# Four small moves of work between engines and queues in a two-layer decoder trunk

## The chip, the cores and the metric

The kernel runs on one core of one Trainium2 chip. The metric is device time in microseconds (us) of one execution, the median of several runs. Five engines work side by side, each with its own instruction stream: TensorE (PE, matmul), VectorE (DVE), ScalarE (ACT), GpSimd (POOL) and SyncE (SP, which here only issues DMAs). They synchronise by semaphores. ACT and SP issue DMAs from their own queues, in the order of their streams.

## The reference

One inference step of a two-layer decoder trunk, in float32, for a prompt of 1024 tokens and 8 sample tokens that share the weights (1032 columns in all). The model width is 1024, the width of the feed-forward part 3072.

```
for l in range(2):
    hn = rmsnorm(x, norm_mix_g[l])
    if l == 0:  main = rglru(conv4(hn @ w_in_a)) * gelu(gate)
    else:       main = window-128 attention over the shared K/V
    mo = memory attention (4 heads, 256 positions)
    x = x + concat(main, mo) @ w_out[l]
    hn = rmsnorm(x, norm_ffn_g[l])
    x = x + conv_ffn(hn, state, w_ffn_up[l], cw, cb, w_ffn_down[l])
    if l == 0:  k_sh, v_sh = shared_kv(x)

def conv_ffn(x, buf, w_up, cw, cb, w_down):
    u = x @ w_up
    u, nbuf = causal_dwconv(u, buf, cw, cb)      # three taps along the tokens
    return (gelu(u[..., :3072]) * u[..., 3072:]) @ w_down, nbuf
```

For a sample token the two earlier columns of the conv come from a saved state, and the last two columns of the prompt and each sample's column are outputs too (`nbuf`).

## The kernel before

**Layout.** Activations lie transposed: 128 features on the partitions, 1032 token columns along the free dimension. A `row` is one tile of 128 x 1032 float32, `sm` and `ty` are smaller ones. `ul` collects the tails of the conv: for each of the 48 up tiles the last two prompt columns and the eight sample columns.

**Matmuls in three passes.** Every float32 operand is split into a high part in a shorter format (`acopy`, made by ACT) and a low part (the difference, made by POOL with `gtt` or DVE with `vtt`). `mm3` (lines 298 to 303) multiplies high x high, high x low and low x high. In the trace these are lines 301, 302 and 303. Lines 108, 116, 119 and 122 are the one-line helpers `act`, `vtt`, `gtt` and `stt`, so most of the work of ACT, DVE and POOL has the line of a helper.

**Up projection.** For each of 24 column tiles `j` of the feed-forward part, `ffn` computes a gate and a value tile together, by seven products of half-sized blocks in place of eight (`STEADY` order P1, P6, P2, P7, P5, P4, P3). `combine` makes the weight of each product from the raw halves: POOL adds or subtracts two 128x512 halves (not for all), ACT copies the high part, POOL subtracts for the low part. The products' sums are added by DVE and copied by ACT into the gate row `ug` and the value row `uv`. After P4 the value row, and after P3 the gate row, is scaled by the norm factor on DVE (`scale`). `post(j)` is a generator that continues one step at each product: conv row of the value (`act_conv`, ACT, with the tail copy), two taps (`taps`, DVE, 128x1023 and 128x1022), the same for the gate, then gelu (ACT), the product of both (DVE), and the store to DRAM (`gD`, by ACT's queue). So a round of one `j` has four taps and two tail copies. After every twelfth `j`, `samples` computes the sample columns from `ul` with four POOL operations, a gelu and a POOL product, and stores them to `gD`.

**Down projection.** While the last column tile is computed, `fetch(i)` loads the first six gated rows back from `gD` and `gated(i)` splits them (high on ACT, low on DVE). The down weights are split by `get` (which loads with `load_w` what is not yet loaded). `down(c, m, b)` then accumulates chunks of six tiles.

**Mixer of layer 1 and its out projection.** Attention results go to DRAM (`mD`). `load_m(b)` loads column block `b` (384, 384 and 264 columns) back and splits it. `start_m(b)` starts that as a task, `mgetB` is asked for a block by the out projection and starts it if it isn't running, then finishes it.

**What sets the order.** The Tile framework schedules DVE, POOL, PE and SP from the program's text; ACT, except in layer 1's mixer, keeps the order in which the program is written. `tick()` advances each running task (`spawn`) by one step. Waits stand in the engine's stream, so what follows a waiting instruction on the same engine or queue waits too.

Of the kernel before, what the change touches and what calls it, by code (L numbers as in the profile page):

```python
# [16 lines left out]
SEQ = 1024  # L17
NB = 8
NT = SEQ + NB
# [10 lines left out]
TIL = ((0, 1, 2), (3, 4, 5), (6, 7))  # L30
# [6 lines left out]
DCH = 6  # L37
SG = 12
# [14 lines left out]
def tile_trunk(ctx: ExitStack, tc: tile.TileContext, I: dict, O: list):  # L53
    nc = tc.nc
    mul, add, sub, amax = ALU.mult, ALU.add, ALU.subtract, ALU.max
# [22 lines left out]
    def row(dt=F32):  # L78
        return rp.tile([P, NT], dt, tag="row", name=nm("row"))
# [30 lines left out]
    def acopy(out, in_, **kw):  # L110
        return act(out, in_, AF.Copy, **kw)

    V, G, T, SY = nc.vector, nc.gpsimd, nc.tensor, nc.sync

    def vtt(out, a, b, op):
        return V.tensor_tensor(out=out, in0=a, in1=b, op=op)  # L116
# [12 lines left out]
    def f(ap):  # L129
        return ap.bitcast(F32)  # L130
# [22 lines left out]
    def spawn(g):  # L153
        t = Task(g)
        tasks.append(t)
        return t
# [75 lines left out]
    gD = dp.tile([2, KF, P, NT], F32, name="gD")  # L232
# [6 lines left out]
    widx = {}  # L239
# [10 lines left out]
    def w_load(i):  # L250
        u = W[i]
        u["raw"] = row()
        a, b = u["shape"]
        SY.dma_start(u["raw"][:, : a * b].rearrange("p (a b) -> p a b", a=a), u["src"])
# [18 lines left out]
    def get(key, ahead=1, load=1):  # L273
        i = widx[key]
        if Prep.fences and i >= Prep.fences[0]:
            Prep.fences.pop(0)
        end = (Prep.fences[0] if Prep.fences else len(W)) - 1
        top = min(end, i + ahead)
        while Prep.split <= top:
            while Prep.loaded <= min(end, Prep.split):  # L280
                w_load(Prep.loaded)
                Prep.loaded += 1
            w_split(Prep.split)
            Prep.split += 1
        while Prep.loaded <= min(end, top + load):
            w_load(Prep.loaded)
            Prep.loaded += 1
        return W[i]["t"]

    def load_w(n):  # L290
        while Prep.loaded < n:
            w_load(Prep.loaded)
            Prep.loaded += 1
# [588 lines left out]
    def ffn(l, ops, need, factor, weights, on_block, store=None):  # L882
        ul3 = ul.rearrange("p (c t) -> p c t", c=10)
# [7 lines left out]
        def act_conv(u, t):  # L891
            a = row()
            act(a[:, :SEQ], u[:, :SEQ], AF.Identity, scale=fwc(2, t), bias=fbc(t))
            G.tensor_copy(out=ul3[:, :, t], in_=u[:, SEQ - 2 : NT])  # L894
            return a

        def taps(a, u, t):
# [23 lines left out]
        def samples(j0):  # L921
            pair = []
            for t0 in (j0, KF + j0):
                t = sm()[:, : 8 * SG].rearrange("p (b j) -> p b j", b=8)
                w = fw[:, None, 2 * MU + t0 : 2 * MU + t0 + SG].to_broadcast([P, 8, SG])
                gtt(t, ul3[:, 2:10, t0 : t0 + SG], w, mul)
                gtt(t, t, sb3[:, :, t0 : t0 + SG], add)
                pair.append(t)
            act(pair[0], pair[0], AF.Gelu_apprx_tanh)
            o = sm()[:, : 8 * SG].rearrange("p (j b) -> p j b", b=8)  # L930
            gtt(o.rearrange("p j b -> p b j"), pair[0], pair[1], mul)
            SY.dma_start(gD[l, j0 : j0 + SG, :, SEQ:NT].rearrange("j p b -> p j b"), o)

        def product(j, name, hfs):
            w = made[j, name]
# [46 lines left out]
        gh, gl, ga = {}, {}, {}  # L982
# [5 lines left out]
        def gated(j):  # L988
            a = ga.pop(j)
            gh[j], gl[j] = row(F32R), row(F32R)  # L990
            acopy(gh[j][:, :NT], a[:, :NT])
            vtt(gl[j][:, :NT], a[:, :NT], f(gh[j][:, :NT]), sub)

        def refill(m):
            x[m] = row()
# [6 lines left out]
        for q, (j, name, hfs) in enumerate(SEQUENCE):  # L1002
            if q == 2:
                load_pair(1)
            if q == 8:
                factor()
            want = 7 + max(0, q - 4) // 2 if q < 14 else min(len(todo), q - 7 + AHEAD)
            while at < want:
                combine(*todo[at])
                at += 1  # L1010
            t = product(j, name, hfs)
            if t is not None:
                last.append(t)
            tick()
            if j == KF - 1:
                i = STEADY.index(name)
                if i < DCH:
                    fetch(i)
                if i > 1:
                    gated(i - 2)  # L1020
                if i == 4:
                    get(f"dn{l}.0.0", 0, 1)

        def down(c, m, b):
# [275 lines left out]
    for i in range(9):  # L1300
        np_ = P if i < 8 else NB
        p = ps()
# [15 lines left out]
    for key in ORDER_A:  # L1318
        t = int(key[1])
# [279 lines left out]
    for j, i in enumerate(order0):  # L1599
        p = ps()  # L1600
# [82 lines left out]
    for i in range(9):  # L1683
        p = ps()
# [15 lines left out]
    swa_done = set()  # L1700
# [133 lines left out]
    sst = None  # L1834
    for e in range(2):
        qu = [get(f"q{e}.{u}", 0, 1) for u in range(4)]
        for j, i in enumerate(order2):
            np_ = P if i < 8 else NB
            p = ps()
            tm(p, 18 + 9 * e + j, qu, 2, 384)  # L1840
            t = start(q_post(p, np_, i, e))
            if i == 8 and e == 1:
# [4 lines left out]
                sst = bgadd(sample_swa(bm96))  # L1847
# [23 lines left out]
    mload = {}  # L1871

    def start_m(b):
        if b not in mload:
            while not {(i, e) for i in TIL[b] for e in range(2)} <= swa_done:
                tick()
            if b == 2:
                bgfinish(sst)
            mload[b] = spawn(load_m(b))
# [7 lines left out]

    x = {}
    start_m(0)
    get("out1.0.0", 1, 1)  # L1890
    for _ in range(6):
        tick()
# [139 lines left out]
```

## Time and profile before

| | us |
|---|---|
| median of 3 runs | 2558.35 |
| the three runs | 2557.54, 2558.35, 2558.95 |
| profiled execution, its own time | 2557.26 |
| profiled execution, span | 2555.5 |
| mean granted TensorE clock | 0.971 |
| busy: PE, DVE, ACT, POOL | 2344.0, 1703.8, 1120.4, 1541.3 |
| up projection layer 0, layer 1 | about 480 to 975, 1780 to 2270 |
| out projection of layer 1 | about 1625 to 1750 |

The span is the time from the first to the last instruction in the trace; times in the trace count from its start. In the rows below a bracket such as [0.60 <-ACT row L108] says that the engine sat idle for 0.60 us before the instruction, until ACT finished a `row` at line 108. The clock is in parts of full speed: 1.00 is 2.4 GHz, 0.50 is 1.2 GHz. "x2" joins two instructions that follow each other; their common time runs from the first's start to the last's end. An instruction's time includes what it waits inside the engine.

### The profile page before, as it was taken

The page shows a single profiled execution, that of the slowest core. Times are in us where ns is not written, and L with a number is a line of the kernel's source. Part 1 is how long each engine was busy: PE and PEld are TensorE (multiplying, and loading weights), DVE is VectorE, ACT ScalarE, POOL GpSimd, SP SyncE. Part 2 cuts the span into 40 slices and gives each one's busy share as a digit, 9 for nine tenths or more (in the row PEclk, how much of TensorE's full clock was granted, in tenths as well). Part 3 has the DMA queues.
Part 4 walks back from the last instruction along what each step waited for, and adds up shares of the span by engine and source line. Part 5 has one row for each costly group of instructions (what it writes and reads, how often), then busy time and mean ns, then how long its engine had stood idle before and what let it go on. Part 6 is the DMA issues. An engine that isn't in the chain of part 4 may idle for free.

```text
span 2555.5 us, 42979 instructions
## 1 busy us (share of the span) xinstructions
PE 2344.0 (92%) x16590; PEld 2250.7 (88%) x16590; DVE 1703.8 (67%) x2772; ACT 1120.4 (44%) x2313; POOL 1541.3 (60%) x1103
## 2 busy tenths in 40 slices
PE   7998879999999998999989987779999999989999
PEld 5898769999999998999977877779999899989999
DVE  6659976777777777332487799777777777773321
ACT  5667865433333334211365577554333333342110
POOL 2149855689999995222144446355899989963220
PEclk9999889999999999999989999889999999999999
DMA  4221134212222216332665553542122222154211
GB/s 162 86 68 46 62 133 135 75 67 75 75 75 75 75 67 236 100 100 76 198 222 161 176 172 105 163 141 94 68 71 71 74 75 72 70 197 147 95 58 64
DMA packets 151132, 273.66 MB, mean 107 GB/s; under 512 B 37184, under 2 KB 93072, under 8 KB 150928
## 3 DMA queue, kind: packets, MB, share of 16 engines
q1 hardware_dynamic: 134800, 237.29, 28.2%
q10 hardware_dynamic: 16128, 33.63, 3.4%
q8 instruction: 131, 2.15, 0.3%
q14 instruction: 73, 0.60, 0.1%
HBM read 211.99 MB, written 58.87 MB: 106 GB/s over the span
## 4 chain that ended last, share of the span: by engine, by line
PE 32%; POOL 30%; issue 13%; DVE 11%; ACT 5%; DMA 1%; SPq 0%; POOLq 0%; ACTq 0%; DVEq 0%
POOL row L119 27%; PE ps L303 10%; PE ps L301 10%; PE ps L302 10%; ACT row L108 4%; DVE row L116 3%; POOL ul L894 2%; DVE row L122 2%; DVE sm L116 2%; DVE ty L116 1%; ACT sm L108 1%; POOL sm L119 1%; DVE ty L399 1%; DVE row L1209 1%; DVE ty L122 0%
## 5 line engine op out<-in xcount | busy, mean ns | idle before, releaser
L301 PE MATMUL ps<-row,row 128*128 128x258 f32 (+4 forms) x5032 | 1512.7, 302 | 47.9 <-ACT row L108 42.8
L303 PE MATMUL ps<-row,row 128*128 128x258 f32 (+4 forms) x5032 | 1493.3, 301 | 49.0 <-POOL row L119 48.7
L302 PE MATMUL ps<-row,row 128*128 128x258 f32 (+4 forms) x5032 | 1508.2, 301 | 26.1 <-DVE row L116 19.0
L119 POOL TENSOR_TENSOR row<-row,row 128x512 fp32r<-128x512 f32 (+9 forms) x666 | 1105.7, 1671 | 688.6 <-ACT row L108 381.5
L301 PEld LDWEIGHTS ps<-row,row 128*128 128x128 f32 x5032 | 957.6, 190 | 71.3 <-ACT row L108 48.4
L303 PEld LDWEIGHTS ps<-row,row 128*128 128x128 f32 x5032 | 951.2, 191 | 67.7 <-POOL row L119 60.8
L302 PEld LDWEIGHTS ps<-row,row 128*128 128x128 f32 x5032 | 958.7, 191 | 40.7 <-DVE row L116 22.4
L108 ACT ACTIVATE row<-row 128x512 fp32r<-128x512 f32 (+9 forms) x688 | 487.3, 738 | 980.5 <-POOL row L119 369.8
L116 DVE TENSOR_TENSOR row<-row,ps 128x258 f32<-128x258 f32 (+2 forms) x672 | 287.2, 444 | 467.7 <-PE ps L303 464.8
L116 DVE TENSOR_TENSOR row<-row,row 128x1032 f32<-128x1032 f32 (+8 forms) x286 | 388.8, 1371 | 110.9 <-ACT row L108 95.3
L122 DVE SCALAR_TENSOR_TENSOR row<-row,fw,row 128x1023 f32<-128x1023 f32 x192 | 349.8, 1841 | 60.9 <-POOL ul L894 47.8
L108 ACT ACTIVATE row<-ps 128x258 f32<-128x258 f32 (+6 forms) x430 | 157.7, 406 | 75.7 <-PE ps L303 26.3
L119 POOL TENSOR_TENSOR row<-row,ty 128x768 f32<-128x768 f32 (+2 forms) x56 | 77.1, 1377 | 165.7 <-DVE ty L416 62.6
L119 POOL TENSOR_TENSOR row<-row 128x512 f32<-128x512 f32 x96 | 163.3, 1701 | 6.7
L108 ACT ACTIVATE row<-row,fw 128x1024 f32<-128x1024 f32 x96 | 114.2, 1230 | 13.1 <-DVE row L116 13.1
L116 DVE TENSOR_TENSOR sm<-sm,sm 128x258 f32<-128x258 f32 (+5 forms) x125 | 90.2, 724 | 32.1 <-ACT sm L108 29.2
L108 ACT ACTIVATE row<-ps,ty,ty 128x256 f32<-128x256 f32 (+1 forms) x160 | 87.4, 563 | 9.1 <-DVE ty L116 7.0
L108 ACT ACTIVATE sm<-ps 128x384 f32<-128x384 f32 (+5 forms) x156 | 65.1, 444 | 41.0 <-PE ps L434 23.7
L116 DVE TENSOR_TENSOR row<-ps,row 128x384 fp32r<-128x384 f32 (+2 forms) x125 | 63.4, 518 | 18.7 <-ACT sm L108 8.4
L894 POOL COPY ul<-row 128x10 f32<-128x10 f32 x96 | 67.8, 706 | 9.2 <-DVE row L116 9.2
L119 POOL TENSOR_TENSOR sm<-sm,row 128x192 f32<-128x192 f32 (+3 forms) x72 | 48.9, 694 | 37.8 <-DVE sm L116 18.3
L122 DVE SCALAR_TENSOR_TENSOR row<-sm,pack,row 128x384 f32<-128x384 f32 (+1 forms) x54 | 59.1, 1097 | 14.0 <-POOL row L127 13.4
(171 smaller groups left out, 1586.8 us busy)
## 6 DMA issues: line engine op xcount, KB each, us to landing
row<-in_w_ffn_up SPq DMA_DIRECT2D x96, 512.0 KB
row<-gD SPq DMA_DIRECT2D x48, 516.0 KB
gD<-row ACTq DMA_DIRECT2D x48, 512.0 KB
row<-in_w_ffn_down SPq DMA_DIRECT2D x64, 384.0 KB
row<-hD SPq DMA_DIRECT2D x48, 512.0 KB
row<-in_w_out SPq DMA_DIRECT2D x32, 512.0 KB
rD<-sm ACTq DMA_DIRECT2D x64, 129.0 KB
row<-rD SPq DMA_DIRECT2D x16, 516.0 KB
```

What stands on the lines that cost most here:

```text
L108: return nc.scalar.activation(out, in_, func, **kw)
L116: return V.tensor_tensor(out=out, in0=a, in1=b, op=op)
L119: return G.tensor_tensor(out=out, in0=a, in1=b, op=op)
L122: return V.scalar_tensor_tensor(out=out, in0=a, scalar=s, in1=b, op0=op0, op1=op1)
L301: T.matmul(out, ah, bh, start=first and j == 0, stop=False, skip_group_check=more)
L302: T.matmul(out, ah, bl, start=False, stop=False, skip_group_check=more)
L303: T.matmul(out, al, bh, start=False, stop=last and j == n - 1, skip_group_check=more)
L399: V.tensor_reduce(out=mx[:, c0 : c0 + m], in_=s3, axis=AX.X, op=amax, negate=True)
L894: G.tensor_copy(out=ul3[:, :, t], in_=u[:, SEQ - 2 : NT])
L1209: V.tensor_tensor_scan(out=y[:, s], data0=r[:, s], data1=gx[:, s], initial=init, op0=mul, op1=add)
```

## The change

Five edits. (A) The tail copies into `ul` go from POOL to ACT, right behind the conv row. (B) Of the first six gated rows of each layer, the low part of rows 0, 2 and 4 is made by POOL and no longer by DVE. (C) The store of the sample columns goes from SP's queue to ACT's. (D) The first two down weights are loaded three products earlier, and the first one is split one product later. (E) In layer 1 a task started with the out projection's first block watches for the attention results of blocks 1 and 2 and starts their loads as soon as these are there, not when the out projection asks for them.

```diff
         def act_conv(u, t):
             a = row()
             act(a[:, :SEQ], u[:, :SEQ], AF.Identity, scale=fwc(2, t), bias=fbc(t))
-            G.tensor_copy(out=ul3[:, :, t], in_=u[:, SEQ - 2 : NT])
+            acopy(ul3[:, :, t], u[:, SEQ - 2 : NT])
             return a
...
             gtt(o.rearrange("p j b -> p b j"), pair[0], pair[1], mul)
-            SY.dma_start(gD[l, j0 : j0 + SG, :, SEQ:NT].rearrange("j p b -> p j b"), o)
+            nc.scalar.dma_start(gD[l, j0 : j0 + SG, :, SEQ:NT].rearrange("j p b -> p j b"), o)
...
             acopy(gh[j][:, :NT], a[:, :NT])
-            vtt(gl[j][:, :NT], a[:, :NT], f(gh[j][:, :NT]), sub)
+            (gtt if j < DCH and j % 2 == 0 else vtt)(gl[j][:, :NT], a[:, :NT], f(gh[j][:, :NT]), sub)
...
                 if i > 1:
                     gated(i - 2)
-                if i == 4:
+                if i == 1:
+                    load_w(widx[f"dn{l}.0.0"] + 2)
+                if i == 5:
                     get(f"dn{l}.0.0", 0, 1)
...
     x = {}
     start_m(0)
+
+    def ask_m():
+        for b in (1, 2):
+            while b not in mload:
+                if {(i, e) for i in TIL[b] for e in range(2)} <= swa_done and (b == 1 or sst.done):
+                    start_m(b)
+                else:
+                    yield
+
+    spawn(ask_m())
     get("out1.0.0", 1, 1)
```

What POOL has in its stream in one regular round of layer 0's up projection before, from the low part of one product's weight to that of a later one (`ul_102` is the tail tile, `row_967` and `row_971` the value and gate row of the round):

```order
L119 TENSOR_TENSOR row_979_6200<-row_954_5899,row_979_6200 128x512
L894 COPY ul_102<-row_967_6064 128x10
L119 TENSOR_TENSOR row_980_6230<-row_954_5899,row_980_6230 128x512
L119 TENSOR_TENSOR row_954_5899<-row_954_5899 128x512
L894 COPY ul_102<-row_971_6098 128x10
L119 TENSOR_TENSOR row_983_6269<-row_955_5901,row_983_6269 128x512
L119 TENSOR_TENSOR row_987_6303<-row_955_5901,row_987_6303 128x512
L119 TENSOR_TENSOR row_991_6337<-row_954_5899,row_991_6337 128x512
```

And the same place on POOL with the change, and below it ACT's stream there:

```order
L119 TENSOR_TENSOR row_979_6200<-row_954_5899,row_979_6200 128x512
L119 TENSOR_TENSOR row_980_6230<-row_954_5899,row_980_6230 128x512
L119 TENSOR_TENSOR row_954_5899<-row_954_5899 128x512
L119 TENSOR_TENSOR row_983_6269<-row_955_5901,row_983_6269 128x512
L119 TENSOR_TENSOR row_987_6303<-row_955_5901,row_987_6303 128x512
L119 TENSOR_TENSOR row_991_6337<-row_954_5899,row_991_6337 128x512
```

```order
L108 ACTIVATE row_980_6230<-row_954_5899 128x512
L108 ACTIVATE row_981_6260<-row_967_6064,fw_100 128x1024
L108 ACTIVATE ul_102<-row_967_6064 128x10
L108 ACTIVATE row_982_6265<-row_971_6098,fw_100 128x1024
L108 ACTIVATE ul_102<-row_971_6098 128x10
L108 ACTIVATE row_983_6269<-row_955_5901 128x512
```

The two copies have left POOL, and the split that stood behind the second (`row_983`) now follows the combine directly; on ACT each copy stands behind its conv row. The rest of the round is in the same order on every engine.

SP's stream before, where the loads of block 2 (`row_2928` and on, from `mD_88`) stand, behind the loads of out weights and of the residual (`xD_87`):

```order
L254 DMA row_2925_18542<-in_w_out 128x1024
L564 DMA row_2926_18544<-xD_87 128x124
L565 DMA row_2926_18544<-xD_87 128x3x128
L568 DMA row_2926_18544<-xD_87 128x8
L564 DMA row_2926_18544<-xD_87 128x124
L565 DMA row_2926_18544<-xD_87 128x3x128
L568 DMA row_2926_18544<-xD_87 128x8
L1860 DMA row_2928_18552<-mD_88 128x2x128 x2
L1860 DMA row_2929_18560<-mD_88 128x2x128 x2
L1860 DMA row_2930_18568<-mD_88 128x2x128 x2
L1860 DMA row_2931_18576<-mD_88 128x2x128 x2
```

And with the change, from the last attention store of layer 1 on:

```order
L1714 DMA mD_88<-sm_2841_18009 128x384
L1862 DMA row_2861_18119<-mD_88 128x2x128 x2
L254 DMA row_2864_18127<-in_w_out 128x1024
L1862 DMA row_2869_18169<-mD_88 128x2x128 x2
L1862 DMA row_2874_18212<-mD_88 128x2x128 x2
L254 DMA row_2877_18220<-in_w_out 128x1024
L560 DMA row_2878_18222<-xD_87 128x4x128
L561 DMA row_2878_18222<-xD_87 128x4
L560 DMA row_2878_18222<-xD_87 128x4x128
L561 DMA row_2878_18222<-xD_87 128x4
L1862 DMA row_2886_18280<-mD_88 128x2x128 x2
```

The eight loads of block 2 moved ahead, to right behind the last attention store and in among the out weights and residual rows of the first half; before, some twenty other DMAs stood between that store and them. The twelve loads of block 1 stand where they stood.

POOL at the end of layer 0's up projection, with the change (128x1032 are the low parts of gated rows 0, 2 and 4; 128x768 those of down weights; 128x96 and 128x8x12 the samples):

```order
L119 TENSOR_TENSOR row_1319_10329<-row_1280_9887,row_1319_10329 128x512
L119 TENSOR_TENSOR row_1322_10362<-row_1311_10287,row_1321_10361 128x1032
L119 TENSOR_TENSOR row_1330_10429<-row_1320_10359,row_1329_10428 128x1032
L119 TENSOR_TENSOR row_1335_10466<-row_1317_10324,row_1334_10465 128x768
L119 TENSOR_TENSOR sm_1344_10520<-ul_102,fw_100 128x96
L119 TENSOR_TENSOR sm_1345_10523<-ul_102,fw_100 128x96
L119 TENSOR_TENSOR sm_1344_10520<-sm_1344_10520,sb_101 128x96
L119 TENSOR_TENSOR sm_1345_10523<-sm_1345_10523,sb_101 128x96
L119 TENSOR_TENSOR row_1339_10505<-row_1328_10426,row_1338_10504 128x1032
L119 TENSOR_TENSOR sm_1346_10527<-sm_1344_10520,sm_1345_10523 128x8x12
L119 TENSOR_TENSOR row_1350_10537<-row_1318_10326,row_1349_10536 128x768
```

Before, the three rows of 128x1032 stood on DVE, two tail copies stood behind the 128x768 split, and the sample product followed the four sample operations directly.

## Rows read from the trace of the kernel before

**Rows 1.** The page, part 1: busy time, share of the span, instructions.
```profile
PE 2344.0 (92%) x16590; PEld 2250.7 (88%) x16590; DVE 1703.8 (67%) x2772; ACT 1120.4 (44%) x2313; POOL 1541.3 (60%) x1103
```

**Rows 2.** Stretches: us; busy of PE, PEld, DVE, ACT, POOL; PEclk; DMA share, GB/s.
```profile
480.00:975.00 495.00, 469.82 (x3808) 460.44 (x3808) 366.40 (x388) 193.97 (x325) 451.96 (x300) 1.00 0.22 75
1690.00:1704.00 14.00, 4.71 (x22) 4.71 (x23) 13.06 (x17) 7.29 (x17) 10.05 (x9) 0.51 0.39 116
```

**Rows 3.** The page, part 5: groups (count | busy us, mean ns | idle before, releaser).
```profile
L303 PE MATMUL ps<-row,row 128*128 128x258 f32 (+4 forms) x5032 | 1493.3, 301 | 49.0 <-POOL row L119 48.7
...
L894 POOL COPY ul<-row 128x10 f32<-128x10 f32 x96 | 67.8, 706 | 9.2 <-DVE row L116 9.2
```

**Rows 4.** Timeline of one round, DVE (start us, duration us, instruction, [idle before]).
```profile
614.27 2.27 DVE L122 SCALAR_TENSOR_TENSOR row<-row,fw,row 128x1023 f32<-128x1023 f32 x1 [1.33 <-POOL ul L894]
616.58 2.20 DVE L122 SCALAR_TENSOR_TENSOR row<-row,fw,row 128x1022 f32<-128x1022 f32 x1
616.58 3.39 DVE L122 SCALAR_TENSOR_TENSOR row<-row,fw,row 128x1022 f32<-128x1022 f32 x2
...
620.56 1.66 DVE L122 SCALAR_TENSOR_TENSOR row<-row,fw,row 128x1022 f32<-128x1022 f32 x1
...
635.81 2.27 DVE L122 SCALAR_TENSOR_TENSOR row<-row,fw,row 128x1023 f32<-128x1023 f32 x1 [1.33 <-POOL ul L894]
```

**Rows 5.** Timeline of the same round, POOL.
```profile
615.54 2.15 POOL L119 TENSOR_TENSOR row<-row 128x512 f32<-128x512 f32 x1
617.64 1.20 POOL L894 COPY ul<-row 128x10 f32<-128x10 f32 x1
618.79 4.58 POOL L119 TENSOR_TENSOR row<-row,row 128x512 fp32r<-128x512 f32 x2
623.97 3.08 POOL L119 TENSOR_TENSOR row<-row,row 128x512 fp32r<-128x512 f32 x2 [0.60 <-ACT row L108]
```

**Rows 6.** Timeline of the same round, ACT.
```profile
611.89 1.16 ACT L108 ACTIVATE row<-row 128x512 fp32r<-128x512 f32 x2 [4.36 <-POOL row L119]
...
622.31 1.58 ACT L108 ACTIVATE row<-row 128x1024 f32<-128x1024 f32 x2 [5.42 <-DVE row L122]
```

**Rows 7.** Timeline of a round halfway, DVE (first three) and POOL.
```profile
745.84 6.55 DVE L122 SCALAR_TENSOR_TENSOR row<-row,fw,row 128x1023 f32<-128x1023 f32 x3 [3.55 <-ACT row L108]
...
752.98 1.63 DVE L122 SCALAR_TENSOR_TENSOR row<-row,fw,row 128x1022 f32<-128x1022 f32 x1
...
768.20 2.27 DVE L122 SCALAR_TENSOR_TENSOR row<-row,fw,row 128x1023 f32<-128x1023 f32 x1 [1.33 <-POOL ul L894]
...
747.78 1.28 POOL L119 TENSOR_TENSOR row<-row 128x512 f32<-128x512 f32 x1
749.02 4.50 POOL L119 TENSOR_TENSOR row<-row,row 128x512 fp32r<-128x512 f32 x2
756.36 1.83 POOL L119 TENSOR_TENSOR row<-row,row 128x512 fp32r<-128x512 f32 x1 [2.83 <-ACT row L108]
```

**Rows 8.** Tile `ul`: who waited for it (us, times).
```profile
DVE row L122: 47.8, 36
```

**Rows 9.** Timeline at block 2 of layer 1's out projection, PE, SP, POOL.
```profile
1699.29 0.58 PE L301 MATMUL ps<-row,row 128*128 128x258 f32 x1 [12.65 <-ACT row L108]
...
1690.86 4.72 SPq L1860 DMA_DIRECT2D row<-mD  x8
...
1689.61 4.48 POOL L119 TENSOR_TENSOR row<-row,row 128x516 fp32r<-128x516 f32 x2
```

**Rows 10.** Timeline from up to down, layer 0, PE and DVE.
```profile
987.38 0.45 PE L302 MATMUL ps<-row,row 128*128 128x384 f32 x1 [1.69 <-DVE row L116]
...
994.90 0.69 PE L301 MATMUL ps<-row,row 128*128 128x384 f32 x1 [3.63 <-ACT row L108]
...
988.57 1.42 DVE L116 TENSOR_TENSOR row<-row,row 128x1032 fp32r<-128x1032 f32 x1
```

**Rows 11.** Groups of POOL, by form (count | busy us, mean ns | idle before).
```profile
L119 POOL TENSOR_TENSOR row<-row,row 128x1032 f32<-128x1032 f32 x6 | 14.9, 2488 | 9.6 <-ACT row L108 5.7 <-DVE row L122 3.8
```

## The prediction

> **What bounds the kernel now.** I read the shares by engine, then one stage of each kind by stretches, then the timeline of one round of the long stage on POOL, DVE and ACT, and last the idle times of PE. PE is busy for 92% of the span, so at first sight little is left [rows 1]. But in the stage that matters most, the up projections (480 to 975 us in layer 0, and its like in layer 1), POOL is busy for 451.96 of 495 us [rows 2], and PE's matmuls of the third kind (line 303) wait 48.7 us in all for POOL's rows [rows 3]. POOL looks like the second bound.
>
> The timeline of one round says otherwise. A round is one of the 24 column tiles of a layer. It repeats from the first tap at 614.27 to the next at 635.81: 21.54 us [rows 4]. In it no engine is full; they wait for each other in a ring. ACT starts its pair at 611.89 after 4.36 us idle, waiting for POOL, and then makes the two conv rows. DVE's four taps run from 614.27 to 620.56 + 1.66 = 622.22. ACT starts the gelu at 622.31 after 5.42 us idle, waiting for DVE. POOL starts its next series at 623.97 after 0.60 us idle, waiting for ACT [rows 4 to 6]. So a round is the sum of POOL's series, DVE's four taps (7.95 us) and ACT's pieces between them. What is removed from POOL outside that sum only makes its idle longer.
>
> Inside the four taps DVE and POOL hold each other up. POOL's 128x512 instruction takes 2.15 us at 615.54, while the same form took 1.28 us at 747.78 [rows 5, 7]. Taps 1 and 2 take 2.27 and 2.20 us; taps 2 and 3 together take 3.39, so tap 3 adds only 1.19 [rows 4]. They take turns: each waits for the other's instruction that is running. The Trainium skill (SBUF - State Buffer, "Who interferes with whom") calls this pair of ports an exclusive lock, held for the whole instruction; the trace agrees with its 2.15 against 1.28 us.
>
> **Part A, the tail copies to ACT.** The copies are 96, with a mean of 706 ns on POOL, 67.8 us in all [rows 3]. The two of a round take 1.41 us, of which the second takes 1.20 [rows 5]. But that copy is mostly waiting: it begins at 617.64 and ends at 618.84, just after tap 2 ends at 616.58 + 2.20 = 618.78. It has POOL's turn and does almost nothing with it, and so tap 3 runs right behind tap 2, unhindered. The order shows that after the change POOL's next split stands there. It takes the turn at 618.78, holds it, and tap 3 has to wait, as taps 1 and 2 do.
>
> What that costs has two prices. By counting turns, tap 3 goes from 1.19 to the 2.27 us of tap 1: +1.08 per round. The other price is measured: in one round halfway, from 745.84, the copies happen to fall before the second tap, and splits stand where the second copy otherwise is. There the first three taps take 6.55 us instead of 614.27 to 619.97 (5.70), and the four last from 745.84 to 752.98 + 1.63 = 754.61, 8.77 us (against 7.95: +0.82). POOL's idle time before its next series grows from 0.60 to 2.83 us, and the next round begins 22.36 us later (768.20) instead of 21.54 [rows 4, 5, 7]. That is the pattern that I expect everywhere. I take 0.88, a quarter of the way from the measured 0.82 to the counted 1.08.
>
> Regular rounds are those whose first tap waits 1.33 us with the copy as the last to come; there are 36 [rows 4, 8]. 36 x 0.88 = **+31.7 us** (29.5 to 38.9). The other 12 (first and last rounds of a layer, and the two that have the pattern already) I take at nothing.
>
> The copies on ACT: no row shows this form there. POOL's first copy of a round took 1.41 - 1.20 = 0.21 us, and two of that lie in ACT's idle 5.42 us [rows 6]; cost nothing. Were that cover gone, 0.21 on the path of 36 rounds would be +7.6.
>
> **Part E, the watcher.** Block 2 of layer 1's out projection finds PE idle for 12.65 us until 1699.29. SP issues that block's eight loads only from 1690.86 [rows 9]. The order shows them now ahead, among the weight loads of the first half; block 1's loads stay where they were, and so does its wait. At most the whole idle time goes, and with it the slow matmuls behind it: from 1690 to 1704 the granted clock is 0.51, and 22 matmuls take 4.71 us, 0.214 each, where the long stage has 469.82 / 3808 = 0.123 [rows 2]; 22 x 0.09 = 2.0. So at most -14.7. What is late next: the low half of the block's second weight, which POOL finishes at 1689.61 + 4.48 = 1694.09 [rows 9]. PE would come from 1686.64 and have 48 matmuls (two tiles of 24) on the first weight, 5.9 us, until 1692.5: a wait of 1.6. I allow three such waits in the block's eight tiles: **-9.9 us**. A loss is not excluded: the eight issues, 4.72 us, now stand ahead of weight loads on SP, and ACT, in written order, may wait for a landing; so +4.7 to -14.7.
>
> **Parts B, C, D, the change from up to down in each layer.** PE waits there 1.69 us for DVE's last splits and 3.63 us for ACT (layer 0) [rows 10]. B moves three of the six splits to POOL, 2.49 us each there (from the nearest form, 128x1032) against 1.42 on DVE [rows 10, 11]. The order puts two of them before the first weights' low half, which is covered by DVE's own splits, and the third behind four sample operations and ahead of the sample product. With C, ACT's queue waits for that product before it can split the next down weight, for which PE already waits 3.63 us. I take two differences of 2.49 - 1.42 = 1.07 on the path per layer, **+4.3 us** in two layers. Ends: both waits vanish, 2 x (1.69 + 3.63) = -10.6; two whole POOL splits are added, 2 x 2 x 2.49 = +10. D's earlier load and later split move under work that PE has anyway: nothing. The Trainium skill (Perfetto Trace Analysis, "Optimizing Scalar/DVE Operations") says that moving work between DVE and GpSimd might not help; by that this part would be 0 and the sum 2579. No row shows these splits on POOL at this place.
>
> **Sum.** 2557.26 (the profiled execution; the median of the runs is 1.1 higher) + 31.7 - 9.9 + 4.3 = 2583.4: **2583 us**.
>
> **Rivals.**
> 1. *POOL is the bound* and the copies' time comes back. For: its 451.96 of 495 us and PE's 48.7 us of waits for it [rows 2, 3]. 36 x 1.41 = 50.8, capped by those 48.7: 2557.3 - 48.7 - 9.9 + 4.3 = 2503. Against: POOL waits for ACT in each round, and where its copies were out of the way its idle grew by 2.2 us and the round did not shrink [rows 5, 7]. 5%. The Trainium skill (Perfetto Trace Analysis, "Optimizing GPSIMD Operations") says to prefer other engines over GpSimd where possible; by that rule this rival would win.
> 2. *The turn is not taken*: the split behind the copy waits for a row of ACT. It decides at 618.78: if ACT's row (now behind two copies) comes later than that, tap 3 runs free and the round stays at 21.54. Then only E and the transitions count: 2557.3 - 9.9 + 4.3 = 2552, faster. Against: that split starts at 618.79 with no idle time before it [rows 5]. 11%.
> 3. *The bubble only moves*: A as forecast, but ACT or SP passes the wait on to the first half. 2557.3 + 31.7 + 4.3 = 2593. For it: ACT takes its queue in order. 19%.
>
> **How the numbers follow.** The forecast has 63%, the rivals 35, mishaps at either end 2. About 0.2% (5 us) can be told from no change. The bounds of the forecast are not all met at once: E and the transitions at their better ends with A at its lower make 2561, and A at its upper with E at nothing and the transitions at +10 make 2606. From 2558 to 2601 the range leaves out rivals 1 and 2 and a little at the top. Faster by over 0.2%: rival 1 and half of rival 2, 0.11. Within: the other half and the lowest of the forecast, 0.07. Slower: 0.82.
>
> **What would show it.** Right: rounds of 22.4 us; tap 3 at 2.2 us or more; POOL's idle time before its series near 2.8 us; PE's waits for POOL longer, not shorter; no copies in POOL's rows and 96 on ACT of about 0.2 us; the idle time at block 2 down to a few us, block 1's wait still there. Wrong: rounds of 21.5 with tap 3 near 1.2 (rival 2), rounds near 20.2 with POOL free of idle time (rival 1), or new PE waits for ACT between 1640 and 1690 (rival 3).

## The result and the profile after

The changed kernel takes 2600.6 us (median of 4 runs, 2597.30 to 2608.73), the kernel before 2558.65 in the same comparison: ratio 1.0169, 95% interval [1.0145, 1.0193], or +37 to +49 us. Slower was forecast, but by 26 us. The time lies at the very end of the range, and the ratio's middle, 2558.65 x 1.0169 = 2602, just beyond it.

The page's first part, of the profiled execution (2608.73 us, the slowest of the four, 8 us above their median; all rows of the changed kernel are from it):

```profile
PE 2365.1 (91%) x16590; PEld 2265.4 (87%) x16590; DVE 1735.7 (67%) x2766; ACT 1129.2 (43%) x2409; POOL 1501.6 (58%) x1013
```

POOL lost 40 us of work against [rows 1], and the time rose. One regular round of layer 0, timeline, DVE first, then POOL, ACT and PE (start us, duration us, instruction, [idle before]):

```profile
619.97 6.63 DVE L122 SCALAR_TENSOR_TENSOR row<-row,fw,row 128x1023 f32<-128x1023 f32 x3 [1.33 <-ACT ul L108]
...
627.19 1.63 DVE L122 SCALAR_TENSOR_TENSOR row<-row,fw,row 128x1022 f32<-128x1022 f32 x1
...
642.42 6.62 DVE L122 SCALAR_TENSOR_TENSOR row<-row,fw,row 128x1023 f32<-128x1023 f32 x3 [1.33 <-ACT ul L108]
...
626.52 0.74 DVE L116 TENSOR_TENSOR row<-row,ps 128x258 f32<-128x258 f32 x2
...
621.11 2.15 POOL L119 TENSOR_TENSOR row<-row 128x512 f32<-128x512 f32 x1
623.22 4.52 POOL L119 TENSOR_TENSOR row<-row,row 128x512 fp32r<-128x512 f32 x2
630.57 4.45 POOL L119 TENSOR_TENSOR row<-row,row 128x512 fp32r<-128x512 f32 x3 [2.83 <-ACT row L108]
...
619.77 0.20 ACT L108 ACTIVATE ul<-row 128x10 f32<-128x10 f32 x1
...
628.91 1.58 ACT L108 ACTIVATE row<-row 128x1024 f32<-128x1024 f32 x2 [6.13 <-DVE row L122]
...
626.99 0.39 PE L301 MATMUL ps<-row,row 128*128 128x258 f32 x1 [0.88 <-DVE row L116]
```

The first three taps take 6.63 us where they took 5.70 [rows 4]; all four take 627.19 + 1.63 - 619.97 = 8.85, before 7.95. POOL's split follows its combine at 623.22 with no copy between. POOL then idles 2.83 us before its next series, before 0.60 [rows 5], and the next round's taps begin 22.45 us later, before 21.54. It is the picture of the halfway round [rows 7] in the regular rounds. The copies on ACT take 0.20 us each and cost nothing, as the second experiment shows.

The longer round reaches PE through DVE. Right behind the third tap DVE adds two matmul results (`ps`, 128x258, at 626.52) to their rows, and PE, which waits for the first of these sums, stands still for 0.88 us. In the round of [rows 4] PE has no such wait. In the whole program it shows at line 301, first before, then after (count | busy us, mean ns | idle before, releasers):

```profile
L301 PE MATMUL ps<-row,row 128*128 128x258 f32 (+4 forms) x5032 | 1512.7, 302 | 47.9 <-ACT row L108 42.8 <-DVE row L116 4.0 <-PE ps L397 1.0
...
L301 PE MATMUL ps<-row,row 128*128 128x258 f32 (+4 forms) x5032 | 1519.2, 304 | 73.6 <-DVE row L116 37.1 <-ACT row L108 36.4
```

PE's waits there for DVE's rows grew from 4.0 to 37.1 us, while those for POOL at line 303 stayed, 48.7 [rows 3] before and 47.9 after.

To place the time, I took from each trace when the n-th matmul starts (the same matmul in all kernels, except that neighbours are swapped in up to some 400 of the 16590 places) and summed differences to the kernel before by stage, in us. "Up" and "to down" are the up projection and the change from up to down of layers 0 and 1, "mixer B" is what lies between layer 0's down projection and layer 1's out projection; the down stages, not shown, moved by 0.2 at most in layer 0 and 0.4 in layer 1.

```
profiled execution       start   up 0  to down 0  mixer B  out proj 1   up 1  to down 1
changed kernel            -1.6   21.4     5.0       3.7      -2.0       19.4     5.5
A alone                   -2.7   20.1    -0.4       1.8       4.5       17.6     1.2
A and an extra copy       -4.0   -1.2    -0.1      -2.8       0.4        0.7     0.3
E alone                   -2.9    0.0    -0.2      -1.5      -5.8        2.6     0.3
E, later                  -3.0   -0.1    -0.2      -1.7      -9.5        2.2    -0.7
E, low parts on POOL      -2.6    0.0     0.0      -0.6      -3.1        1.6    -0.8
B, C, D                   -2.3    0.3     6.2      -1.4      -0.3        1.4     8.1
B alone                   -2.7    1.1     6.6       2.2       4.2        0.0     6.8
C alone                   -0.7    0.3     4.2      -2.0       5.4        0.9     3.5
rows 0 and 2, C, D        -2.2    1.0     6.2       0.0       4.9        0.9     6.4
E later, rows 0 and 2     -0.3    0.3     0.1      -0.9      -9.5        1.7     0.8
changed, two undone       -3.4   20.1     1.7       0.4      -1.1       18.2     2.1
```

The start and the mixer are the same work in all of these, and vary by up to 4 and 6.5 us; differences below that, in these two columns, mean nothing. Where nothing in them was changed, the up stages repeat within 3 us and the changes to down within 2.

The out projection varies by 5 us even where nothing in it was changed, and this has a place. In seven of the thirteen traces (the changed kernel; A; B; C; rows 0 and 2, C, D; E, low parts on POOL; changed, two undone) its first 85 matmuls take 3.9 to 5.5 us longer than in the kernel before. In these seven PE, some 40 matmuls into the stage, waits 1.8 to 2.1 us for DVE, and in or right behind that wait the granted clock falls to 0.50. In the other traces these matmuls differ by 0.5 us at most. An example of the wait, then the 6.7 us around and behind it, and the same place with E alone (us; PE busy (matmuls), PEclk, DMA share, GB/s):

```profile
1640.97 0.58 PE L302 MATMUL ps<-row,row 128*128 128x258 f32 x1 [2.04 <-DVE row L116]
1640.20:1646.90 6.70, 5.38 (x23) 0.50 0.11 40
...
1638.20:1644.90 6.70, 6.70 (x52) 1.00 0.37 108
```

From the 86th matmul to the end of the out projection all kernels without part E agree with the kernel before within 0.1 us, and those with it gain 6.3 (E alone), 5.9 (changed kernel and changed, two undone), 9.5 (E, later), 9.4 (E later, rows 0 and 2) and 8.6 us (E, low parts on POOL).

The out projection of layer 1 (timeline; DVE, ACT, PE):

```profile
1698.71 4.69 DVE L116 TENSOR_TENSOR row<-row,row 128x264 fp32r<-128x264 f32 x4
1703.33 0.41 DVE L116 TENSOR_TENSOR sm<-row,ps 128x258 f32<-128x258 f32 x1
...
1703.77 0.51 ACT L108 ACTIVATE row<-sm,pack 128x258 f32<-128x258 f32 x1 [5.68 <-DVE sm L116]
...
1705.59 0.58 PE L301 MATMUL ps<-row,row 128*128 128x258 f32 x1 [5.61 <-ACT row L108]
```

The 12.65 us before block 2 [rows 9] are gone, and a wait of 5.61 us stands in the first half, where there was none of that size. Following the chain back: PE waits for a weight's high part on ACT; ACT, in written order, stands before a sum's scaling that waits for DVE; DVE makes four of block 2's low parts first (4.69 us).

The change from up to down, layer 0 (PE, then POOL, then DVE and ACT):

```profile
1013.86 0.69 PE L302 MATMUL ps<-row,row 128*128 128x384 f32 x1 [5.92 <-POOL row L119]
...
1020.52 0.45 PE L301 MATMUL ps<-row,row 128*128 128x384 f32 x1 [2.26 <-ACT row L108]
...
1006.28 2.54 POOL L119 TENSOR_TENSOR sm<-ul,fw 128x96 f32<-128x96 f32 x2 [4.57 <-ACT ul L108]
1008.78 2.70 POOL L119 TENSOR_TENSOR sm<-sm,sb 128x96 f32<-128x96 f32 x2
1011.44 2.36 POOL L119 TENSOR_TENSOR row<-row,row 128x1032 fp32r<-128x1032 f32 x1
...
1015.92 0.56 DVE L116 TENSOR_TENSOR row<-row,ps 128x384 f32<-128x384 f32 x1 [4.69 <-PE ps L303]
...
1019.62 4.22 ACT L108 ACTIVATE row<-row 128x768 fp32r<-128x768 f32 x5 [7.06 <-DVE row L116]
```

POOL makes row 4's low part (128x1032) only after four sample operations, and PE waits 5.92 us for it. DVE's sums then wait for PE, the last gated row behind these sums, and ACT's next weight behind that row's store. Before, PE waited 1.69 and 3.63 us here [rows 10].

### The profile page after: what moved, and what is told of

Same layout as the page of the kernel before. It is cut to its first block, busy times and chain, and to the rows that moved or that the text cites. A ratio compares the mean times of both kernels' runs of the same rounds, so it can differ in the third digit from the quotient of the medians.

```text
span 2606.9 us, 43020 instructions
## 1 busy us (share of the span) xinstructions
PE 2365.1 (91%) x16590; PEld 2265.4 (87%) x16590; DVE 1735.7 (67%) x2766; ACT 1129.2 (43%) x2409; POOL 1501.6 (58%) x1013
## 5 line engine op out<-in xcount | busy, mean ns | idle before, releaser
L301 PE MATMUL ps<-row,row 128*128 128x258 f32 (+4 forms) x5032 | 1519.2, 304 | 73.6 <-DVE row L116 37.1
L119 POOL TENSOR_TENSOR row<-row,row 128x512 fp32r<-128x512 f32 (+11 forms) x672 | 1124.3, 1686 | 784.2 <-ACT row L108 461.1
L302 PE MATMUL ps<-row,row 128*128 128x258 f32 (+4 forms) x5032 | 1515.8, 303 | 31.7 <-DVE row L116 15.4
L303 PE MATMUL ps<-row,row 128*128 128x258 f32 (+4 forms) x5032 | 1498.9, 302 | 48.1 <-POOL row L119 47.9
L116 DVE TENSOR_TENSOR row<-row,row 128x1032 f32<-128x1032 f32 (+8 forms) x280 | 381.4, 1373 | 96.8 <-ACT row L108 79.0
L122 DVE SCALAR_TENSOR_TENSOR row<-row,fw,row 128x1023 f32<-128x1023 f32 x192 | 387.8, 2040 | 71.4 <-ACT ul L108 51.9
L122 DVE SCALAR_TENSOR_TENSOR row<-sm,pack,row 128x384 f32<-128x384 f32 (+1 forms) x54 | 59.8, 1111 | 14.0 <-POOL row L127 13.4
L108 ACT ACTIVATE row<-sm,pack 128x258 f32<-128x258 f32 x64 | 32.4, 507 | 74.6 <-DVE sm L116 74.6
```

Source lines behind the costliest of these rows:

```text
L108: return nc.scalar.activation(out, in_, func, **kw)
L119: return G.tensor_tensor(out=out, in0=a, in1=b, op=op)
L122: return V.scalar_tensor_tensor(out=out, in0=a, scalar=s, in1=b, op0=op0, op1=op1)
L301: T.matmul(out, ah, bh, start=first and j == 0, stop=False, skip_group_check=more)
L302: T.matmul(out, ah, bl, start=False, stop=False, skip_group_check=more)
L303: T.matmul(out, al, bh, start=False, stop=last and j == n - 1, skip_group_check=more)
```

## The experiments

**Part A alone.** One line of the kernel before, nothing else.

```diff
-            G.tensor_copy(out=ul3[:, :, t], in_=u[:, SEQ - 2 : NT])
+            acopy(ul3[:, :, t], u[:, SEQ - 2 : NT])
```

> Part A alone (the 96 tail copies on ACT, nothing else changed). Turn theory: the split takes the turn that the copy left unused, so the 36 regular rounds go from 21.53 to 22.42 us, third tap 2.3 in place of 1.27, and the total rises by 30 to 34: about 2590. Rival (POOL is the bound and gets its time back): about 2508. Rival (the change's loss comes from its other parts): 2558.

Measured: 2597.82, ratio 1.0154 [1.0139, 1.0169], +39 us. The taps:

```profile
619.00 6.62 DVE L122 SCALAR_TENSOR_TENSOR row<-row,fw,row 128x1023 f32<-128x1023 f32 x3 [1.33 <-ACT ul L108]
...
641.43 4.38 DVE L122 SCALAR_TENSOR_TENSOR row<-row,fw,row 128x1023 f32<-128x1023 f32 x2 [1.33 <-ACT ul L108]
```

Rounds of 22.43 and slow third taps, as the turn theory says; the rivals fall. But the total rose by 39 us and not by 30 to 34, and the up stages by 37.7, not by 36 x 0.89 = 32.0. By the first taps' starts the first round of layer 0 takes 23.67 in place of 21.42 and the last that can be measured 23.12 in place of 21.59; with their like in layer 1 these add 7.1 us, and I had put them at nothing. The fourth round of layer 0, one of the 36, takes 23.68 in place of 21.53, and the twelfth round of each layer, also of the 36, shrinks by 0.4.

**Part A and an extra copy that nothing needs.** This is the direct test: only the turn is given back, not the work.

```diff
+            acopy(ul3[:, :, t], u[:, SEQ - 2 : NT])
-            G.tensor_copy(out=ul3[:, :, t], in_=u[:, SEQ - 2 : NT])
...
             ag = act_conv(ug, j)
+            G.tensor_copy(out=ty()[:, :10], in_=ug[:, SEQ - 2 : NT])
```

> Part A, and beside it one extra copy of 10 columns on POOL into a tile that nothing reads, where the second tail copy stood. Turn theory: a copy with no work gives DVE its turn back; third tap 1.27, rounds 21.53, total 2558 within 3. Rival (the two copies on ACT lengthen the ring, or the conv row is read by two engines): rounds stay at 22.4 and the total at 2590.

Measured: 2559.47, ratio 0.9997 [0.9984, 1.0011].

```profile
611.66 5.56 DVE L122 SCALAR_TENSOR_TENSOR row<-row,fw,row 128x1023 f32<-128x1023 f32 x3 [1.33 <-ACT ul L108]
...
614.90 1.19 POOL L909 COPY ty<-row 128x10 f32<-128x10 f32 x1
616.05 4.58 POOL L119 TENSOR_TENSOR row<-row,row 128x512 fp32r<-128x512 f32 x2
621.22 4.46 POOL L119 TENSOR_TENSOR row<-row,row 128x512 fp32r<-128x512 f32 x3 [0.59 <-ACT row L108]
```

The useless copy takes 1.19 us on POOL, three taps are back at 5.56, POOL idles 0.59 us again, and the next round's taps start at 633.06, 21.40 later. PE's waits at line 301 for DVE's rows are 2.7 us in all, where A alone has 38.3. All of part A's loss is the lost turn; ACT's copies cost nothing. This agrees with the exclusive lock on the ports that DVE and GpSimd share, of which the Trainium skill tells (SBUF - State Buffer, "Who interferes with whom"); that the two engines take turns by the instruction is what the traces add.

**Part E alone.** The watcher, as in the change, in the kernel before.

```diff
     start_m(0)
+    def ask_m():
...
+    spawn(ask_m())
```

> Part E alone (the watcher). Theory 1 (the wait only moves: block 2's low parts on DVE delay the first half's sums, and the in-order ACT with them): the 12.65 us at block 2 go, new waits of 5 us or more appear in the first half, total 2554 to 2557. Theory 2 (E is good for its full 10 us, and what was lost was lost to other parts of the change): total about 2548 and no new wait over 3 us in the first half.

Measured: 2553.66, ratio 0.9981 [0.9970, 0.9991]. As in theory 1 the wait moves, in the same chain as above:

```profile
1662.51 4.69 DVE L116 TENSOR_TENSOR row<-row,row 128x264 fp32r<-128x264 f32 x4
...
1667.57 0.51 ACT L108 ACTIVATE row<-sm,pack 128x258 f32<-128x258 f32 x1 [5.65 <-DVE sm L116]
...
1669.38 0.58 PE L301 MATMUL ps<-row,row 128*128 128x258 f32 x1 [5.66 <-ACT row L108]
```

The out projection gains 5.8 us in this trace, 6.3 behind its first 85 matmuls; by the runs E is worth 5 us (2 to 8).

**The watcher, later.** Part E, with block 2 held back for four more steps.

```diff
                 if {(i, e) for i in TIL[b] for e in range(2)} <= swa_done and (b == 1 or sst.done):
+                    if b == 2:
+                        for _ in range(4):
+                            yield
                     start_m(b)
```

> Part E alone, with the watcher holding block 2 back for four more steps. Theory 1 (the splits of block 2 on DVE, ahead of the first half's sums, hold ACT's queue and through it PE; later they do it less): the new wait in the first half shrinks below 4 us, block 2 still finds its rows ready, total 2549 to 2553. Theory 2 (the wait comes from the loads standing ahead of weight loads on SP): no change against the watcher alone, 2553 to 2556, or the 12.65 us come back in part.

Measured: 2548.24, ratio 0.9970 [0.9958, 0.9982], faster than the kernel before and the changed one, by 0.3% against the kernel before.

```profile
1670.61 0.39 PE L301 MATMUL ps<-row,row 128*128 128x258 f32 x1 [1.49 <-ACT row L108]
```

That is the longest wait left in the first half, apart from the one that starts the stage, and 1.50 us stood there before too. Block 2 still finds its rows. So it is where block 2's work stands, not that it is done early, that cost the difference: 5.8 us are gained in the out projection with the watcher as it is, 9.5 with the later one. The difference rests on the traces; the two ratios' intervals overlap. The four steps hold back the loads as well as the splits, and the next experiment tells them apart.

**Block 2's low parts on POOL.** Part E, with the low parts of block 2 made by POOL.

```diff
-                vtt(Ml[k][:, c0 : c0 + n], r3[:, e], f(Mh[k][:, c0 : c0 + n]), sub)
+                (gtt if b == 2 else vtt)(Ml[k][:, c0 : c0 + n], r3[:, e], f(Mh[k][:, c0 : c0 + n]), sub)
```

> Part E alone, with block 2's eight low parts made by POOL in place of DVE. Theory 1 (DVE's queue carries the wait into the first half): the wait of 5 to 7 us there shrinks to under 3, total 2548 to 2553. Theory 2 (SP's queue or ACT's high parts carry it): it stays, total 2553 to 2557, or worse by POOL's slower splits.

Measured: 2552.53, ratio 0.9980 [0.9970, 0.9989]. The wait of 5.66 us is gone, but PE now waits for POOL there:

```profile
1672.60 0.39 PE L303 MATMUL ps<-row,row 128*128 128x258 f32 x1 [1.94 <-POOL row L119]
...
1680.30 0.40 PE L303 MATMUL ps<-row,row 128*128 128x258 f32 x1 [1.68 <-POOL row L119]
```

The loads stand where they stand with E alone, so the wait came from the splits on DVE, as in theory 1. On POOL they cost less: the first half, behind the first 85 matmuls, loses 2.0 us against 5.6 with E alone, and the out projection from there on gains 8.6 us, not 6.3. The table's -3.1 is smaller because this trace has the second fall of the clock at the stage's start and E alone doesn't. By the runs the total can't be told from E alone: whether that fall is part of the other executions too, no trace shows.

**Parts B, C and D**, tail copies on POOL.

```diff
-            SY.dma_start(gD[l, j0 : j0 + SG, :, SEQ:NT].rearrange("j p b -> p j b"), o)
+            nc.scalar.dma_start(gD[l, j0 : j0 + SG, :, SEQ:NT].rearrange("j p b -> p j b"), o)
...
-            vtt(gl[j][:, :NT], a[:, :NT], f(gh[j][:, :NT]), sub)
+            (gtt if j < DCH and j % 2 == 0 else vtt)(gl[j][:, :NT], a[:, :NT], f(gh[j][:, :NT]), sub)
...
-                if i == 4:
+                if i == 1:
+                    load_w(widx[f"dn{l}.0.0"] + 2)
+                if i == 5:
                     get(f"dn{l}.0.0", 0, 1)
```

> Parts B, C and D together, tail copies still on POOL. Theory 1 (the fifth gated row's low part on POOL, behind four sample operations, is what PE waits for): each layer's change from up to down loses 4 to 6 us, total 2566 to 2570. Theory 2 (it needs the tail copies on ACT too, for which the sample operations wait): at most 2 us lost per layer, total 2558 to 2562.

Measured: 2575.24, ratio 1.0076 [1.0055, 1.0097], +19 us; 6.2 and 8.1 us in the two changes to down, more than theory 1's 4 to 6. Theory 2 falls: the tail copies are not needed for it.

**Part B alone.**

```diff
-            vtt(gl[j][:, :NT], a[:, :NT], f(gh[j][:, :NT]), sub)
+            (gtt if j < DCH and j % 2 == 0 else vtt)(gl[j][:, :NT], a[:, :NT], f(gh[j][:, :NT]), sub)
```

> Part B alone (low parts of gated rows 0, 2, 4 on POOL). Theory 1 (row 4 on POOL behind the four sample operations is the whole loss of B, C and D): PE waits about 6 us for POOL near the end of the up stage, as with B, C and D together; total 2570 to 2577. Theory 2 (the store or the earlier weights cost it): at most 2562.

Measured: 2569.73, ratio 1.0057 [1.0042, 1.0072].

```profile
991.46 0.69 PE L302 MATMUL ps<-row,row 128*128 128x384 f32 x1 [5.53 <-POOL row L119]
```

The wait of theory 1 is there, and 6.6 and 6.8 us are lost in the two changes. By itself it makes 13.4 of the three parts' 14.3 us in the traces, and +15 of their +19 in the runs, whose intervals overlap.

**Rows 0 and 2 alone on POOL, with C and D.** As in the experiment on parts B, C and D, with another choice of rows:

```diff
-            vtt(gl[j][:, :NT], a[:, :NT], f(gh[j][:, :NT]), sub)
+            (gtt if j in (0, 2) else vtt)(gl[j][:, :NT], a[:, :NT], f(gh[j][:, :NT]), sub)
```

> Parts C and D, and B with rows 0 and 2 only; row 4 stays on DVE. Theory 1 (the place behind the sample operations costs it, not POOL's slower split as such): PE's wait of 6 us for POOL goes, total 2553 to 2561, level with the kernel before. Theory 2 (each split on POOL costs its 1 us or more, or C and D cost): 2565 or more.

Measured: 2574.41, ratio 1.0071 [1.0054, 1.0087]: a miss. The wait for POOL is gone, and another one took its place (ACT, then PE):

```profile
994.98 4.84 ACTq L919 DMA_DIRECT2D gD<-row  x1
999.93 4.22 ACT L108 ACTIVATE row<-row 128x768 fp32r<-128x768 f32 x5 [6.75 <-DMA row<-gD]
...
1000.82 0.69 PE L301 MATMUL ps<-row,row 128*128 128x384 f32 x1 [8.95 <-ACT row L108]
```

The store of the last gated row, issued right after the sample store on ACT's queue, takes 4.84 us to issue, and ACT stands still for it. In the changed kernel the same issue takes 0.33 us, because row 4 on POOL has delayed it by 5 us: one loss hides the other. In layer 1 the issue takes 3.37 us here.

**Part C alone.**

```diff
-            SY.dma_start(gD[l, j0 : j0 + SG, :, SEQ:NT].rearrange("j p b -> p j b"), o)
+            nc.scalar.dma_start(gD[l, j0 : j0 + SG, :, SEQ:NT].rearrange("j p b -> p j b"), o)
```

> Part C alone (the sample store issued by ACT). Theory 1 (on ACT's queue the next store of a gated row can only be issued when the sample store's many small pieces are taken in; ACT stands still meanwhile, and the next down weight's split with it): that issue takes 4 to 5 us instead of 0.33, PE's wait of 3.6 us for ACT grows to 8 or 9 in each layer, total 2566 to 2570. Theory 2 (the long issue was chance, or came with the other parts): total 2556 to 2560.

Measured: 2567.12, ratio 1.0027 [1.0016, 1.0038], +7 us (4 to 10).

```profile
993.72 0.40 ACTq L932 DMA_DIRECT2D gD<-sm  x1
994.16 5.12 ACTq L919 DMA_DIRECT2D gD<-row  x1
...
1000.22 0.69 PE L301 MATMUL ps<-row,row 128*128 128x384 f32 x1 [9.12 <-ACT row L108]
```

Theory 1 holds in layer 0 and in part in layer 1: issuing takes 5.12 us here and 2.71 us in layer 1, PE's wait for ACT grows from 3.63 to 9.12 and from 3.91 to 6.75 us. That the sample store's pieces cause it (128 x 12 pieces of 8 columns) is argued; their number was not varied. Part D was never run by itself. Rows 0 and 2 with C and D lose 12.6 us in the two changes to down, C alone 7.7, and rows 0 and 2 without C and D only 0.9 (the last experiment): by difference D may cost up to 4 us, and what it delays is not shown.

**The whole change, with the sample store on SP and row 4 on DVE.** Against the changed kernel:

```diff
-            nc.scalar.dma_start(gD[l, j0 : j0 + SG, :, SEQ:NT].rearrange("j p b -> p j b"), o)
+            SY.dma_start(gD[l, j0 : j0 + SG, :, SEQ:NT].rearrange("j p b -> p j b"), o)
...
-            (gtt if j < DCH and j % 2 == 0 else vtt)(gl[j][:, :NT], a[:, :NT], f(gh[j][:, :NT]), sub)
+            (gtt if j in (0, 2) else vtt)(gl[j][:, :NT], a[:, :NT], f(gh[j][:, :NT]), sub)
```

> The whole change, but with the sample store on SP and gated row 4 on DVE (rows 0 and 2 stay on POOL). Theory 1 (row 4 and the store, each by itself, make the loss at the change from up to down): both layers' waits of 6 us for POOL and of 9 us for ACT are gone, the total falls by 10 to 13 against the whole change: 2588 to 2591. Theory 2 (the tail copies, late on ACT, hold the sample operations and with them the rest): the total stays at 2597 to 2601.

Measured: 2596.42, ratio 1.0155 [1.0129, 1.0180]. In the traces the changes to down fall from 5.0 and 5.5 us to 1.7 and 2.1, and the waits of 6 us for POOL are gone; a wait of 9 us for ACT was not there to go, since in the changed kernel it was 2.26 us. So theory 1 has the place right, but not the size: 6.7 us in the traces and 4 in the runs, not 10 to 13, and the intervals of the totals overlap. The total lies above theory 1's range and just under theory 2's; that the waits for POOL went with the tail copies still on ACT speaks against theory 2.

**The later watcher, and rows 0 and 2 on POOL**, everything else as before: the two diffs of those experiments together.

```diff
+    def ask_m():
...
+                        for _ in range(4):
+                            yield
...
-            vtt(gl[j][:, :NT], a[:, :NT], f(gh[j][:, :NT]), sub)
+            (gtt if j in (0, 2) else vtt)(gl[j][:, :NT], a[:, :NT], f(gh[j][:, :NT]), sub)
```

> The later watcher, and rows 0 and 2 on POOL; sample store on SP, tail copies on POOL, down weights as before. If rows 0 and 2 on POOL cost nothing where the sample store stays on SP: PE's waits for DVE and ACT at the change from up to down stay at 1 to 4 us each, total 2545 to 2550. If each split on POOL costs its extra 1 us or more on the path: 2551 to 2556.

Measured: 2549.29 against 2559.78, ratio 0.9953 [0.9938, 0.9967].

```profile
988.21 0.44 PE L302 MATMUL ps<-row,row 128*128 128x384 f32 x1 [0.65 <-DVE row L116]
990.88 0.45 PE L302 MATMUL ps<-row,row 128*128 128x384 f32 x1 [0.98 <-DVE row L116]
995.78 0.69 PE L301 MATMUL ps<-row,row 128*128 128x384 f32 x1 [3.68 <-ACT row L108]
```

Two splits on POOL take 1 us off the wait for DVE, and the stage gains nothing (0.1 and 0.8 us): ACT's weight still ends last. The Trainium skill's warning that moving work between DVE and GpSimd might not help (Perfetto Trace Analysis, "Optimizing Scalar/DVE Operations") holds for these two rows. This version and the later watcher alone, whose intervals overlap, are the fastest here; both are faster than the kernel before and the changed one.

## Why the prediction was right and wrong

**What bounds the kernel** held. The round is a ring, not POOL. Rival 1 (POOL is the bound, 2503) is refuted by A alone, and by the idle time of 2.83 us. One sign of being right did not come: PE's waits for POOL were to grow, and at line 303 they are 47.9 us after 48.7. PE loses the time waiting for DVE's sums behind the third tap, 4.0 to 37.1 us at line 301; the prediction had the ring longer, but not where PE would feel it. The Trainium skill's general advice to prefer other engines over GpSimd (Perfetto Trace Analysis, "Optimizing GPSIMD Operations") fails here: following it cost 1.54%. Rival 2 (the turn is not taken) is refuted by the third tap.

**Part A, +31.7.** The mechanism and the price were right: 0.88 per regular round forecast, 22.43 - 21.54 = 0.89 measured, and the extra copy shows that it is the turn. The step that failed in size was "the other 12 I take at nothing": A alone adds 37.7 us in the up stages, of which 36 x 0.89 = 32.0 is the regular rounds'. The first and last rounds of both layers add 7.1 and the fourth of layer 0 1.3 beyond its 0.89; the twelfth rounds, which shrank, take back 2.5. Why these rounds differ is not shown.

**Part E, -9.9.** The 14.7 us at block 2 did go, idle time and slow matmuls. What failed was "what is late next": I allowed three waits of 1.6 us for POOL's weights. There are such waits (0.7 to 1.3 us), but the large new one, 5.6 us, came from DVE: block 2's splits stand ahead of the first half's sums. It is rival 3 in part: ACT passes the wait on, as that rival says, but what holds ACT is DVE, which it doesn't name. E gave 5 us in the runs, and 5.9 in the changed kernel's trace behind the first 85 matmuls.

**Parts B, C and D, +4.3.** This is the step that failed in its mechanism. The order had shown row 4 behind the samples, and I priced it by its duration against DVE's, 1.07 us, and not by when it could start. PE waits 5.9 us for it, because POOL takes its stream in order: first the four sample operations, and these need the last tails. And C was priced as a wait for the product alone, when issuing the next store could take 2.7 to 5.1 us by itself. B alone loses 6.6 and 6.8 us, C alone 4.2 and 3.5, all three together 6.2 and 8.1, and in the changed kernel 5.0 and 5.5: they hide each other, and must not be summed. Even the bound of +10, two whole splits added per layer, was too low. That D costs nothing is open, and by difference unlikely.

**The sum.** Forecast 31.7 - 9.9 + 4.3 = 26. With A and E from the experiments and the changes to down as they stand in the changed kernel, 37.7 - 5.8 + 10.5 = 42.4, against 37 to 49 measured. That it comes so near the middle is partly luck: with the 14.3 us of B, C and D run together it would be 46, and by the runs' totals (+39, -5, +19) 53, so the parts do not add up exactly. The three terms of the forecast missed by 6.0, 4.1 and 6.2 us, all to the same side, and no single one of them explains it. The range's upper end was made of A's upper bound, E at nothing and the changes to down at +10; the time got there with A near that bound, E at little more than half its price and the changes to down just past theirs.

## What to carry to other kernels

Where two engines share a port and take turns, an instruction that does almost nothing can be worth its time: before moving it away, see who takes the turn, and look for a place in the trace where that order already occurs. An instruction that moves to another queue is priced by when its place in that queue comes, not by its duration. Work that is started early is still made by engines in a fixed order; ask ahead of whose instructions it will stand.

## What the runs showed of the hardware

A DMA of one whole row takes 0.33 us to issue from ACT, but 4.84 and 5.12 us in layer 0, and 3.37 and 2.71 in layer 1, soon behind a store of many small pieces on the same queue; with 5 us or more between the two it takes 0.33 to 0.62. On SP, before, the issue after that store took 1.27 us.

A stage whose instructions are untouched can differ by 4 to 6 us between two kernels' profiled executions (the mixer, -2.8 to +3.7), more than the parts that were looked for there. In the out projection the difference goes with a wait of about 2 us and a granted clock of 0.50 behind it, which seven of the thirteen traces have at its start; the untouched part behind that place agrees within 0.1 us.
